# SwiGLU's last 1024 features mostly by seven products, and a last norm scaled on VectorE from PSUM

## The chip, the cores and the metric

One NeuronCore of a Trainium2 chip runs the whole step. The metric is device time in microseconds of one execution. The engines are TensorE (PE; PEld is its weight load), VectorE (DVE), ScalarE (ACT), GpSimd (POOL) and SyncE (SP, which only issues DMAs). All arithmetic is on float32 data; a float32 product is made of three matmuls on operands split into a high and a low part.

## What is computed

One step of a streaming encoder layer on 576 rows (512 of a prompt, 64 of a sample) of width 1024, the inner width of SwiGLU being 4096. The parts that the change touches are the two SwiGLUs and the last norm:

```python
def rmsnorm(x, g):
    y = xf * lax.rsqrt(jnp.mean(xf * xf, axis=-1, keepdims=True) + EPS)
    return y * g
def swiglu(x, w_in, w_out):
    a, b = jnp.split(x @ w_in, 2, axis=-1)
    return (jax.nn.silu(a) * b) @ w_out
# layer
x = x + 0.5 * swiglu(rmsnorm(x, norm_ffn1), w_ffn1_in, w_ffn1_out)
x = x + mixer(rmsnorm(x, norm_mix))        # SSD, band attention, mLSTM, gates, output projection
x = x + 0.5 * swiglu(rmsnorm(x, norm_ffn2), w_ffn2_in, w_ffn2_out)
y = rmsnorm(x, final_norm)
```

## The kernel before, in words

The state lies transposed in SBUF as eight tiles R of 128 features by 576 rows. A float32 operand is split (`split`, L288 and L289) into a rounded high part made by a cast on ScalarE and the rest, subtracted on VectorE; `ph` and `pl` are those of a weight, `XH`/`XL`, `YH`/`YL` and `TH`/`TL` those of data. Three matmuls, (high, high), (high, low) and (low, high), add up in PSUM.

There are two ways to multiply. The plain one (`gemm`, `matmuls`, L260) goes by output tiles of 128 features and two pieces of the rows, `HALVES`, of 256 and 320. The other (`stream`, `product`, L616) is a scheme with seven products in place of eight: a unit makes two output tiles by two halves of 288 rows from two halves of the inner dimension, out of sums of weight quarters (made by an accumulating DMA from GpSimd, L461, and GpSimd additions, L472) and sums of data halves (`operands`, `hidden_operands`). Each of the seven products has four pieces of 128 inner features by three matmuls of 288 columns, and each weight operand is a 128x512 split. `stream` interleaves the products of neighbouring units and prepares weight operands five products ahead; evacuations have a raised priority. Jobs in `jobs` (the splits of hidden tiles) run between products, one step at each `tick`.

`ffn` first makes four of the hidden tiles plainly and then streams: units of the input projection (`unit`, evacuated by `swiglu`, L627 to L643, into `g` tiles of 128x2x288), and, for each 1024 hidden features c = 0, 1, 2, four units `out(c, m)` of the output projection, evacuated by `residual` (L655) into R. For the last 1024 features (c = 3) the hidden tiles are split whole (`hidden_parts`, L681) into YH and YL, whose memory takes the place of the operand tiles T2 after `out(2, 3)` (`hidden_tiles`), and the output projection of these 1024 features is plain: `gemm` in two parts of 512 (`for i in (6, 7)`), evacuated by `evac_o` at L712. The first FFN ("a") ends with rows 0 to 255 and then 256 to 575; the last one ("c", `last=(1, 0)`) the other way round.

After the first FFN the mixer begins with `norm`: per feature tile XH on ScalarE (L338) and XL on VectorE (L339), squares on ScalarE (L296, L299) added up on VectorE (L300), column sums by TensorE (`total`, L314), the power on GpSimd (L306), a spread of the row scales over partitions by TensorE (`spread`, L330) and a copy to `rs` on ScalarE (L354). Plain X tiles of the mixer need only XH and XL; their evacuations (L600) and the seven-product operands (xk at L434, then xd and splits) need `rs`. Then come a gate tile (L1488) and transposes of gates (L794), and the mixer's seven-product units.

After the last FFN, `norm_out` takes the squares, sums and row scales for rows 256 to 575 first (h = 1), copies the spread scales to `rs` (L401) and multiplies the eight tiles at L422, four on VectorE and four on GpSimd. Rows 0 to 255 are transposed (L408), scaled by two engines from PSUM (L413 on VectorE, L415 on ScalarE) and stored row by row. Pools hand memory on from tag to tag: a tile that is allocated where another lay waits for the other's last reader. The scheduler lists each engine's instructions in an order fixed at build time.

Of the kernel before, what the change touches and what calls it, by code (L numbers as in the profile page):

```python
# [35 lines left out]
NB = 63  # L36
NS = 115
# [44 lines left out]
class Hybrid:  # L82
    def __init__(self, ctx, tc, I, O):
# [7 lines left out]
        self.b_i = 0  # L91
        self.jobs, self.gap, self.side = deque(), 0, iter(())
# [102 lines left out]
    def squares(self, tag):  # L195

        pool, bufs = self.sqp
        if pool is self.op:
            return self.op.tile([128, T], F32, name=bufs[tag], tag=bufs[tag], bufs=2)[:, :320]
        return pool.tile([128, 320], F32, name=tag, tag=tag, bufs=bufs[tag])  # L200
# [44 lines left out]
    def parts(self, src):  # L245
        return self.split(src, self.ring("ph", F32R), self.ring("pl", F32R))
# [133 lines left out]
    def norm_out(self, x, g0, out):  # L380

        nc = self.nc
        with self.tc.high_priority(offset=1500):
            for h in (1, 0):
# [25 lines left out]
        for i in range(4):  # L410
            o = self.ring("wr")
            if i % 2:
# [39 lines left out]
    def fetch_sums(self, desc):  # L452
# [5 lines left out]
        src = self.I["sblk"][i].rearrange("p (q c) -> p q c", q=4)  # L458
        x12 = self.ring("wx", shape=(128, 2, 512))
# [3 lines left out]
    def fetch(self, raw):  # L463

        for q in (2, 3, 0) if self.mixer else (0, 2, 3):
            raw[q] = self.ring("wr")
# [20 lines left out]
    def stream(self, seq, order, banks):  # L487
# [17 lines left out]
        for i, (n, t) in enumerate(uses):  # L505
# [11 lines left out]
            if t == self.T_X2:  # L517
                del raw[n], st[n]

    def pairs(self, seq):  # L520
# [26 lines left out]
        def pair(tiles, done):  # L547
# [20 lines left out]
            return (name, 0, c1, c2), self.T, on  # L568
# [40 lines left out]
    def product(self, ps, ops, moving, start):  # L609
# [3 lines left out]
        for kk in range(4):  # L613
            wsl = slice(kk * 128, (kk + 1) * 128)
            for i, (wt, xx) in enumerate(((hi, th), (hi, tl), (lo, th))):
                self.nc.tensor.matmul(ps, wt[:, wsl], xx[:, kk, :], start=(start and kk == 0 and i == 0),  # L616
                                      stop=(kk == 3 and i == 2), skip_group_check=True)
# [62 lines left out]
    def hidden_parts(self, slot, g):  # L680
        self.split(g.rearrange("p h t -> p (h t)"), self.YH[:, slot, :], self.YL[:, slot, :])  # L681
        yield 1

    def ffn(self, x, g0, win, wout, name, last=(0, 1)):

# [24 lines left out]
        def evac_o(ot):  # L710
            def go(h, ps, sl):
                nc.vector.scalar_tensor_tensor(x[:, ot, sl], ps, 0.5, x[:, ot, sl], op0=ALU.mult, op1=ALU.add)  # L712
# [3 lines left out]
        def at(c, j):  # L716
            return (8 * c + (j if c == 3 else j % 2 * 4 + j // 2)) * 128
# [22 lines left out]
        def flush():  # L740
# [3 lines left out]
            for c, j in sorted(got):  # L744
                if c == 3:
                    self.jobs.append(self.hidden_parts(j, got.pop((c, j))))
                elif j % 2 == 0 and (c, j + 1) in got:
                    self.jobs.append(self.hidden_operands(j // 2, got.pop((c, j)), got.pop((c, j + 1))))
# [3 lines left out]
        def unit(c, j):  # L752
# [3 lines left out]
            return (win, 0, 4096 + at(c, j), at(c, j)), self.T, self.swiglu(done)  # L756

        def out(c, m):
            def done():
                free[0] = True  # L760
                if c == 2:
                    self.hidden_tiles(name)
                flush()
            return (wout, 1024 * c, 256 * m, 256 * m + 128), self.T2, self.residual(x, m, done if m == 3 else None)
# [844 lines left out]
```

## Time and profile before

| what | value |
|---|---|
| runs of the kernel | 1943.83, 1940.4, 1938.6 us; median 1940.4 us |
| profiled execution, its own time | 1944.79 us |
| its span on the core | 1943.1 us |
| mean granted clock of TensorE | 0.991 |
| busy: PE, DVE, ACT, POOL | 1887.2, 1524.6, 1089.5, 680.1 us |

The profiled execution is one of many; its time lies a little above the median. Times in the rows are microseconds from the start of the span, unless marked ns. TensorE issues a matmul before the last one has left the array, so a matmul's own duration (about 0.3 us) is longer than the distance to the next. `x12` at a row's end counts instructions of one kind in a row; in brackets is the idle time of the engine before them, and what ended it.

### The profile page before, as it was taken

What the parts mean: (1) busy time and instruction counts of PE and PEld (TensorE: products, weight loads), DVE (VectorE), ACT (ScalarE), POOL (GpSimd) and SP (SyncE); (2) the same over time, 40 slices, a digit from 0 to 9 for tenths busy, and PEclk for the clock granted to TensorE, in tenths of its full rate; (3) what the DMA queues carried; (4) which work ended last, traced back from release to release, by engine and by line L of the source; (5) the groups of instructions that cost most, each with busy time, mean ns of one, the idle gap of its engine ahead of it and who ended that gap; (6) DMA issues with size and microseconds to landing.
All of it is one profiled execution on the core that took longest, in us unless ns stands there. A gap on an engine that the chain in (4) does not pass through costs nothing. (4 is left out here: it accounts for less than half of the span.)

```text
span 1943.1 us, 37678 instructions
## 1 busy us (share of the span) xinstructions
PE 1887.2 (97%) x13901; PEld 1823.6 (94%) x13901; DVE 1524.6 (78%) x2715; ACT 1089.5 (56%) x2486; POOL 680.1 (35%) x656
## 2 busy tenths in 40 slices
PE   9999999999999999999999998999999999999998
PEld 8899999999999878888888888999999999999998
DVE  8998998988768767667777775745898888988865
ACT  4554654655544777767675765324555455554544
POOL 5343333333202234323435353440233334334311
PEclk9999999999999999899999999999999999999999
DMA  7267666666742545753667557742236666666631
GB/s 241 74 160 173 159 163 163 159 172 163 185 131 80 156 117 159 200 147 108 183 165 183 155 152 213 241 143 88 77 99 165 163 157 172 166 157 167 159 94 60
DMA packets 129440, 294.69 MB, mean 152 GB/s; under 512 B 14289, under 2 KB 26193, under 8 KB 129257
## 3 DMA queue, kind: packets, MB, share of 16 engines
q1 hardware_dynamic: 100072, 205.67, 32.7%
q0 software_dynamic: 19696, 72.10, 20.5%
q10 hardware_dynamic: 9488, 14.53, 2.6%
q8 instruction: 109, 1.79, 0.4%
q14 instruction: 75, 0.61, 0.1%
HBM read 272.87 MB, written 19.38 MB: 150 GB/s over the span
## 5 line engine op out<-in xcount | busy, mean ns | idle before, releaser
L616 PE MATMUL acc<-TH,ph 128*128 128x288 f32 x3220 | 968.0, 301 | 27.4 <-ACT uv L533 11.8
L616 PE MATMUL acc<-TL,ph 128*128 128x288 f32 x3220 | 955.4, 297 | 0.6 <-DVE TL L289 0.6
L616 PE MATMUL acc<-TH,pl 128*128 128x288 f32 x3220 | 955.0, 298 | 1.0 <-DVE pl L289 0.9
L616 PEld LDWEIGHTS acc<-TH,ph 128*128 128x128 f32 x3220 | 607.5, 189 | 46.9 <-ACT uv L533 15.5
L616 PEld LDWEIGHTS acc<-TL,ph 128*128 128x128 f32 x3220 | 609.4, 189 | 4.9 <-issue 3.7
L616 PEld LDWEIGHTS acc<-TH,pl 128*128 128x128 f32 x3220 | 608.4, 189 | 4.8 <-DVE pl L289 2.2
L289 DVE TENSOR_TENSOR pl<-wr,ph 128x512 fp32r<-128x512 f32 x471 | 429.4, 919 | 76.9 <-ACT ph L288 64.5
L288 ACT CAST ph<-wr 128x512 fp32r<-128x512 f32 x471 | 287.9, 620 | 267.9 <-PE acc L616 141.3
L289 DVE TENSOR_TENSOR pl<-wx,ph 128x512 fp32r<-128x512 f32 x390 | 328.1, 845 | 44.5 <-ACT ph L288 37.9
L288 ACT CAST ph<-wx 128x512 fp32r<-128x512 f32 x390 | 237.4, 621 | 201.3 <-POOL wx L472 110.2
L472 POOL TENSOR_TENSOR wx<-wx,wr 128x512 f32<-128x512 f32 x160 | 246.3, 1539 | 188.2 <-DVE pl L289 150.4
L461 POOL DMA_DIRECT2D wx<-in_sblk x115 | 101.6, 901 | 524.1 <-DMA wx<-in_sblk 154.7
L260 PE MATMUL acc<-YH,ph 128*128 128x256 f32 (+1 forms) x768 | 226.5, 298 | 6.3 <-ACT YH L288 5.8
L260 PE MATMUL acc<-YL,ph 128*128 128x320 f32 (+1 forms) x768 | 227.1, 297 | 2.3 <-DVE YL L339 1.9
L260 PE MATMUL acc<-YH,pl 128*128 128x256 f32 (+1 forms) x768 | 226.5, 296 | 0.1
L260 PEld LDWEIGHTS acc<-YH,ph 128*128 128x128 f32 x768 | 145.4, 190 | 6.9 <-ACT YH L288 5.9
L260 PEld LDWEIGHTS acc<-YL,ph 128*128 128x128 f32 x768 | 145.4, 189 | 3.5 <-DVE YL L339 3.3
L260 PEld LDWEIGHTS acc<-YH,pl 128*128 128x128 f32 x768 | 145.2, 189 | 0.3 <-DVE pl L289 0.3
L472 POOL TENSOR_TENSOR wy<-wx,wr 128x512 f32<-128x512 f32 x35 | 56.2, 1605 | 136.0 <-DVE pl L289 120.0
L655 DVE SCALAR_TENSOR_TENSOR R<-acc,R 128x288 f32<-128x288 f32 x168 | 75.7, 450 | 18.6 <-PE acc L616 18.1
L288 ACT CAST TH<-g 128x288 fp32r<-128x288 f32 x120 | 51.6, 434 | 59.8 <-POOL g L641 34.6
L289 DVE TENSOR_TENSOR pl<-wy,ph 128x512 fp32r<-128x512 f32 x70 | 59.8, 857 | 29.6 <-ACT ph L288 26.6
(320 smaller groups left out, 2393.4 us busy)
## 6 DMA issues: line engine op xcount, KB each, us to landing
wr<-in_sblk SPq DMA_DIRECT2D x345, 256.0 KB, 3.6
wx<-in_sblk SPq DMA_DIRECT2D x115, 512.0 KB, 3.8
wx<-in_sblk POOLq DMA_DIRECT2D x115, 512.0 KB, 6.8
wr<-in_wblk SPq DMA_DIRECT2D x126, 256.0 KB, 3.0
R<-scr_rows ACTq DMA_DIRECT2D x12, 576.0 KB, 5.9
gs<-g SPq DMA_DIRECT2D x20, 288.0 KB, 4.5
g<-gs POOLq DMA_DIRECT2D x20, 288.0 KB, 3.9
y<-ys POOLq DMA_DIRECT2D x12, 288.0 KB, 3.8
```

Of the source, the lines that this page charges most:

```text
L260: nc.tensor.matmul(ps[:, :n], wt[:, wsl], xx[:, k0 + k, a:a + n], start=(k == 0 and i == 0), stop=(k == nk - 1 and i == 2))
L288: self.nc.scalar.copy(hi, src)
L289: self.nc.vector.tensor_tensor(lo, src, hi.bitcast(F32), op=ALU.subtract)
L461: return {"x12": x12, "src": src}, lambda: nc.gpsimd.dma_start(x12, src[:, 1:3, :], accum_op=ALU.add)
L472: add = lambda o, one, two: self.nc.gpsimd.tensor_tensor(o, one, two, op=ALU.add)
L616: self.nc.tensor.matmul(ps, wt[:, wsl], xx[:, kk, :], start=(start and kk == 0 and i == 0), stop=(kk == 3 and i == 2), skip_group_check=True)
L655: self.nc.vector.scalar_tensor_tensor(o, ps, scale, o, op0=ALU.mult, op1=ALU.add)
```

## The change

Of the last 1024 hidden features, 768 (six hidden tiles, three pairs) now go by seven products like the others: `out(3, m)`, four units with three pieces of 128 in each product (`product` takes their number from the operand's width; the weight quarters are 128x384, filled with zeros to 512 in HBM and loaded at 384). The other 256 (hidden tiles j = 6, 7) stay plain: `rest(m, n)` runs between the units, right behind the last product of each, with one 128x512 weight split in a unit (loaded into a `g` buffer) and four pieces of 288 columns of 6 matmuls; the banks are those of the stream. `hidden_parts` splits tiles 6 and 7 into piece 3 of the operand tiles of T_X1, T_A11, T_X4 and T_A22, which the three-piece products leave free. The pool of YH and YL is no longer opened in their place, so T2 lives until the end of the FFN. The plain `gemm` calls at the end are gone.

In `norm_out` the spread scales stay in PSUM, all eight multiplications of rows 256 to 575 are on VectorE, behind the last residual (`issue_after(self.final)`), and of the four last scalings one, not two, is on VectorE. The squares take buffers of the weights (`wr`) and of `g`.

```diff
@@ norm_out
                 if h:
                     self.total([acc], n, pt)
-                    ps, _ = self.spread(pt, n)
-                    rb = self.rs[:, :320]
-                    nc.scalar.copy(rb, ps[:, :n])
+                    rb = self.spread(pt, n)[0][:, :n]
...
-            if i % 2:
+            if i == 1:
                 nc.vector.tensor_scalar(o, tr[i], r[:, i // 2:i // 2 + 1], None, op0=ALU.mult)
...
         for k in range(8):
-            eng = nc.gpsimd if k % 2 else nc.vector
-            eng.tensor_tensor(x[:, k, sl], x[:, k, sl], rb, op=ALU.mult)
+            with self.tc.issue_after(self.final):
+                nc.vector.tensor_tensor(x[:, k, sl], x[:, k, sl], rb, op=ALU.mult)
@@ stream, product
+            if self.then:
+                self.then = self.then()
...
-        for kk in range(4):
+        nk = hi.shape[1] // 128
+        for kk in range(nk):
@@ hidden tiles
-    def hidden_parts(self, slot, g):
-        self.split(g.rearrange("p h t -> p (h t)"), self.YH[:, slot, :], self.YL[:, slot, :])
-        yield 1
+    def rest(self, k, h):
+
+        return [v[:, 3, :] for v in self.T2[(self.T_X1, self.T_A11, self.T_X4, self.T_A22)[2 * k + h]]]
+
+    def hidden_parts(self, k, g):
+        for h in range(2):
+            self.split(g[:, h, :], *self.rest(k, h))
+            yield 1
@@ ffn
+        def rest(m, n):
+
+
+            late.append(self.parts(raws.pop(0)))
+            if m < 2:
+                todo = [(m, e, h) for e in range(2) for h in range(2)]
+            else:
+                todo = [(g, e, h) for h in last for g in (2, 3) for e in range(2) if (g == 2 and h == last[0]) == (m == 2)]
...
+            for g, e, h in todo:
+                hi, lo = late[g]
+                ps = self.half_bank(banks.pop())
+                for k in range(2):
+                    th, tl = self.rest(k, h)
+                    wsl = slice(k * 256 + e * 128, k * 256 + e * 128 + 128)
+                    for i, (w, t) in enumerate(((hi, th), (hi, tl), (lo, th))):
+                        nc.tensor.matmul(ps, w[:, wsl], t, start=(k == 0 and i == 0), stop=(k == 1 and i == 2))
+                evac_o(2 * g + e)(h, ps, slice(h * FH, (h + 1) * FH))
+
+        def out(c, m, n=None):
             def done():
+                if c == 3:
+                    self.then = partial(rest, m, n)
+                    return
                 free[0] = True
-                if c == 2:
-                    self.hidden_tiles(name)
                 flush()
...
+        seq += [out(3, m, len(seq) + m) for m in range(4)]
...
-        for i in (6, 7):
-            tiles = [((wout, i * 512, 512, j * 256, 256), [(0, evac_o(2 * j)), (128, evac_o(2 * j + 1))])
-                     for j in range(4)]
-            n = 1 if i == 7 else 4
-            self.gemm(tiles[:n], self.YH, self.YL, k0=(i % 2) * 4)
-            self.gemm(tiles[n:], self.YH, self.YL, k0=(i % 2) * 4, half_major=True, order=last)
+        self.sqp = self.wp, None
```

The scheduler puts the instructions in an order of its own. Where the first FFN ends and the mixer's norm begins, VectorE's list before reads as follows (L712 are the residuals of the plain tiles, L339 the XL of the mixer, L289 subtractions of weight splits, L300 sums of squares):

```order
L339 SCALAR_TENSOR_TENSOR XL<-R_60,cst,XH 128x320
L712 SCALAR_TENSOR_TENSOR R_60<-acc,R_60 128x320
L289 TENSOR_TENSOR pl<-wr,ph 128x512
L712 SCALAR_TENSOR_TENSOR R_60<-acc,R_60 128x320
L339 SCALAR_TENSOR_TENSOR XL<-R_60,cst,XH 128x320
L289 TENSOR_TENSOR pl<-wr,ph 128x512
L300 TENSOR_TENSOR xd<-xd,xk 128x256 x2
```

And after, where the same steps are L727 (residuals of `rest`), L663 (residuals of the units), L345 (XL), L295 and L306:

```order
L727 SCALAR_TENSOR_TENSOR R_60<-acc,R_60 128x288 x2
L295 TENSOR_TENSOR pl<-wr,ph 128x512
L727 SCALAR_TENSOR_TENSOR R_60<-acc,R_60 128x288 x2
L295 TENSOR_TENSOR pl<-wr,ph 128x512
L345 SCALAR_TENSOR_TENSOR XL<-R_60,cst,XH 128x256 x2
L306 TENSOR_TENSOR xd<-xd,xk 128x256
L345 SCALAR_TENSOR_TENSOR XL<-R_60,cst,XH 128x256 x2
L306 TENSOR_TENSOR xd<-xd,xk 128x256
L345 SCALAR_TENSOR_TENSOR XL<-R_60,cst,XH 128x256 x4
```

Before, XL and residuals alternate; after, the XL stand behind the last residual.

On TensorE, the list at the same place goes before from the plain tiles of YH to those of XH:

```order
L260 MATMUL acc<-YH,ph 128x320
L260 MATMUL acc<-YL,ph 128x320
L260 MATMUL acc<-YH,pl 128x320
L260 MATMUL acc<-XH,ph 128x256
L260 MATMUL acc<-XL,ph 128x256
L260 MATMUL acc<-XH,pl 128x256
```

After, from the last piece of `rest` (L803; the operand tiles TH_907 to TL_910 are those that hold hidden tiles 6 and 7) to the X tiles:

```order
L803 MATMUL acc<-TH_907,ph 128x288
L803 MATMUL acc<-TL_908,ph 128x288
L803 MATMUL acc<-TH_907,pl 128x288
L803 MATMUL acc<-TH_909,ph 128x288
L803 MATMUL acc<-TL_910,ph 128x288
L803 MATMUL acc<-TH_909,pl 128x288
L266 MATMUL acc<-XH,ph 128x256 x3
L266 MATMUL acc<-XL,ph 128x256
L266 MATMUL acc<-XH,pl 128x256
```

The X matmuls follow directly in both. Counted in the lists, the second spread of the norm (L330, after: L336) stands behind 118 matmuls of X tiles before, and behind 172 after.

At the kernel's end, VectorE's list before (L422 the scalings of rows 256 to 575, L305 and L325 first steps of the power, L413 the last scalings):

```order
L712 SCALAR_TENSOR_TENSOR R_60<-acc,R_60 128x256
L300 TENSOR_TENSOR na<-na,sq 128x256 x2
L712 SCALAR_TENSOR_TENSOR R_60<-acc,R_60 128x256
L300 TENSOR_TENSOR na<-na,sq 128x256 x2
L712 SCALAR_TENSOR_TENSOR R_60<-acc,R_60 128x256
L300 TENSOR_TENSOR na<-na,sq 128x256 x2
L422 TENSOR_TENSOR R_60<-R_60,rs 128x320 x4
L712 SCALAR_TENSOR_TENSOR R_60<-acc,R_60 128x256
L305 TENSOR_SCALAR sm<-ps_x 128x2
L413 TENSOR_SCALAR wr<-acc,sm 128x512 x2
```

And after (L426 the scalings, L311 and L331 the first steps, L417 the last scaling):

```order
L663 SCALAR_TENSOR_TENSOR R_60<-acc,R_60 128x288
L727 SCALAR_TENSOR_TENSOR R_60<-acc,R_60 128x288 x2
L306 TENSOR_TENSOR wr<-wr,g 128x320 x2
L306 TENSOR_TENSOR wr<-wr,g 128x256 x3
L311 TENSOR_SCALAR sm<-ps_x 128x2
L331 TENSOR_SCALAR sm<-ps_x 64x1
L306 TENSOR_TENSOR wr<-wr,g 128x256 x3
L426 TENSOR_TENSOR R_60<-R_60,ps_x 128x320 x8
L311 TENSOR_SCALAR sm<-ps_x 128x2
L417 TENSOR_SCALAR wr<-acc,sm 128x512
```

The last residual moved ahead of the scalings, of which there are eight, and the sums of squares stand behind it too.

## Rows read from the trace of the kernel before

**Rows 1.** Table of windows: PE, PEld, DVE, ACT, POOL busy, granted clock, DMA.
```profile
200.00:400.00 200.00, 199.67 (x1496) 199.21 (x1495) 182.93 (x282) 111.62 (x236) 76.27 (x68) 1.00 0.64 164
500.00:520.00 20.00, 20.00 (x152) 20.00 (x151) 17.32 (x24) 11.92 (x24) 6.00 (x6) 1.00 0.65 170
600.00:620.00 20.00, 20.00 (x152) 20.00 (x151) 20.00 (x36) 8.96 (x17) 6.98 (x4) 1.00 0.25 84
628.00:630.00 2.00, 2.00 (x11) 1.50 (x10) 2.00 (x5) 1.05 (x2) 0.00 (x0) 0.60 0.00 0
1880.00:1930.00 50.00, 50.00 (x377) 49.85 (x375) 27.34 (x58) 21.00 (x42) 2.15 (x3) 1.00 0.13 38
```

**Rows 2.** Chain of waits, its last 180 us: start, duration, engine, tile, line.
```profile
1763.66 110.58 PE acc L616 x828
1881.02 44.58 PE acc L260 x331
1925.60 0.55 PE ps_x L314 x6
1926.14 3.48 PE acc L260 x28
1929.63 0.82 PE ps_x L330 x6
1930.47 0.44 ACT rs L401
1930.97 4.39 POOL R L422 x4
```

**Rows 3.** The page's costliest groups, whole kernel: busy us, mean ns, idle before.
```profile
L289 DVE TENSOR_TENSOR pl<-wr,ph 128x512 fp32r<-128x512 f32 x471 | 429.4, 919 | 76.9 <-ACT ph L288 64.5
L289 DVE TENSOR_TENSOR pl<-wx,ph 128x512 fp32r<-128x512 f32 x390 | 328.1, 845 | 44.5 <-ACT ph L288 37.9
L472 POOL TENSOR_TENSOR wx<-wx,wr 128x512 f32<-128x512 f32 x160 | 246.3, 1539 | 188.2 <-DVE pl L289 150.4
L655 DVE SCALAR_TENSOR_TENSOR R<-acc,R 128x288 f32<-128x288 f32 x168 | 75.7, 450 | 18.6 <-PE acc L616 18.1
```

**Rows 4.** Groups of VectorE by line and shape, whole kernel.
```profile
L289 DVE TENSOR_TENSOR TL<-g,TH 128x288 fp32r<-128x288 f32 x120 | 56.7, 475 | 17.2 <-ACT TH L288 17.2
L289 DVE TENSOR_TENSOR YL<-g,YH 128x576 fp32r<-128x576 f32 x16 | 18.2, 1150 | 1.0 <-ACT YH L288 1.0
L339 DVE SCALAR_TENSOR_TENSOR XL<-R,cst,XH 128x320 fp32r<-128x320 f32 x8 | 4.4, 546 | 1.3 <-ACT XH L338 1.3
L712 DVE SCALAR_TENSOR_TENSOR R<-acc,R 128x320 f32<-128x320 f32 x32 | 15.6, 489 | 12.2 <-PE acc L260 12.1
```

**Rows 5.** Timeline of VectorE, 560 to 640 us: start us, duration us.
```profile
573.96 0.55 DVE L339 SCALAR_TENSOR_TENSOR XL<-R,cst,XH 128x320 fp32r<-128x320 f32 x1
574.42 0.48 DVE L712 SCALAR_TENSOR_TENSOR R<-acc,R 128x320 f32<-128x320 f32 x1
594.81 1.54 DVE L434 SCALAR_TENSOR_TENSOR xk<-R,cst,rs 128x576 f32<-128x576 f32 x2
628.41 0.45 DVE L289 TENSOR_TENSOR TL<-xk,TH 128x288 fp32r<-128x288 f32 x1
```

**Rows 6.** Timeline of TensorE at the hand-over and at the gates.
```profile
575.38 0.31 PE L260 MATMUL acc<-YH,pl 128*128 128x320 f32 x1
575.53 0.28 PE L260 MATMUL acc<-XH,ph 128*128 128x256 f32 x1
625.48 0.30 PE L794 MATMUL ps_x<-ident,R 24*128 24x24 f32 x2 [2.37 <-DVE R L1488]
```

**Rows 7.** Timeline of ScalarE, second copy of row scales in the mixer.
```profile
593.55 0.43 ACT L354 COPY rs<-ps_x 128x320 f32<-128x320 f32 x1 [1.79 <-PE ps_x L330]
```

**Rows 8.** Timeline of VectorE at the kernel's end.
```profile
1930.93 3.71 DVE L422 TENSOR_TENSOR R<-R,rs 128x320 f32<-128x320 f32 x4 [0.25 <-ACT rs L401]
1934.56 0.41 DVE L712 SCALAR_TENSOR_TENSOR R<-acc,R 128x256 f32<-128x256 f32 x1
```

More of the change, by code (lines that the diff above doesn't have):

```diff
@@ L35 @@
 CH = [(0, 128), (128, 128), (256, 128), (384, 128), (512, 64)]
-NB = 63
-NS = 115
+NB = 51
+NS = 123
 FH = 288
@@ L91, in __init__ @@
         self.b_i = 0
+        self.then = None
         self.jobs, self.gap, self.side = deque(), 0, iter(())
@@ L199, in squares @@
             return self.op.tile([128, T], F32, name=bufs[tag], tag=bufs[tag], bufs=2)[:, :320]
+        if pool is self.wp:
+            o = self.ring("wr") if tag == "na" else pool.tile([128, T], F32, name="g", tag="g", bufs=FBUFS["g"])
+            return o[:, :320]
         return pool.tile([128, 320], F32, name=tag, tag=tag, bufs=bufs[tag])
@@ L711, in go @@
             def go(h, ps, sl):
-                nc.vector.scalar_tensor_tensor(x[:, ot, sl], ps, 0.5, x[:, ot, sl], op0=ALU.mult, op1=ALU.add)
+                o = nc.vector.scalar_tensor_tensor(x[:, ot, sl], ps, 0.5, x[:, ot, sl], op0=ALU.mult, op1=ALU.add)
+                self.final = o.ins
             return go
         def at(c, j):
-            return (8 * c + (j if c == 3 else j % 2 * 4 + j // 2)) * 128
+            return (8 * c + (j if c == 3 and j > 5 else j % 2 * (3 if c == 3 else 4) + j // 2)) * 128
         boxes = [{} for _ in range(NPLAIN)]
@@ L744, in flush @@
             for c, j in sorted(got):
-                if c == 3:
-                    self.jobs.append(self.hidden_parts(j, got.pop((c, j))))
+                if c == 3 and j > 5:
+                    self.jobs.append(self.hidden_parts(j - 6, got.pop((c, j))))
+                    for m in (2 * j - 12, 2 * j - 11):
+                        w = self.wp.tile([128, T], F32, name="g", tag="g", bufs=FBUFS["g"])[:, :512]
+                        if m % 2 == 0:
+                            self.plan.append((wout, 3840, 256, m * 256, 512))
+                        nc.sync.dma_start(w, self.I["wblk"][len(self.plan) - 1][:, m % 2 * 512:m % 2 * 512 + 512])
+                        raws.append(w)
                 elif j % 2 == 0 and (c, j + 1) in got:
+                    if c == 3:
+                        self.jobs.append(iter((2,)))
                     self.jobs.append(self.hidden_operands(j // 2, got.pop((c, j)), got.pop((c, j + 1))))
@@ L755, in done @@
                 flush()
-            return (win, 0, 4096 + at(c, j), at(c, j)), self.T, self.swiglu(done)
-        def out(c, m):
+            return (win, 0, 4096 + at(c, j), at(c, j), 4), self.T, self.swiglu(done)
+        raws, late = [], []
+        def rest(m, n):
[4 more added lines that the diff above has]
+                todo = [(g, e, h) for h in last for g in (2, 3) for e in range(2) if (g == 2 and h == last[0]) == (m == 2)]
+            banks = deque((n % 3, 4 + n % 2, 3, (n + 2) % 3) if m < 3 else
+                          (n % 3, 4 + n % 2, 3, (n + 2) % 3, 4 + (n + 1) % 2, (n + 1) % 3))
+            for g, e, h in todo:
[8 more added lines that the diff above has]
+        def out(c, m, n=None):
             def done():
+                if c == 3:
+                    self.then = partial(rest, m, n)
+                    return
                 free[0] = True
-                if c == 2:
-                    self.hidden_tiles(name)
                 flush()
-            return (wout, 1024 * c, 256 * m, 256 * m + 128), self.T2, self.residual(x, m, done if m == 3 else None)
+            return ((wout, 1024 * c, 256 * m, 256 * m + 128, 3 if c == 3 else 4), self.T2,
+                    self.residual(x, m, done if m == 3 or c == 3 else None))
         for j, box in enumerate(boxes):
```

26 lines of the change are left out of this document (16 added, 10 removed).

## The prediction

> **What bounds the kernel now.** I read the table of windows and the chain of waits first, at the places that the change touches, since a removed matmul is worth its issue interval only while TensorE stays fed. In the first feed-forward (FFN) TensorE is busy 199.67 of 200 us in 200 to 400 us and all of 500 to 520 [rows 1]; in the last FFN the chain is one unbroken run of 828 seven-product matmuls in 110.58 us, and then 44.58 us of plain ones [rows 2]. So both places are TensorE's. Only after 1930 us does the chain pass to ScalarE and GpSimd [rows 2]. The third place is the start of the mixer: from 600 to 620 us VectorE is busy 20.00 of 20 us [rows 1], so there VectorE sets when the mixer's seven-product operands are ready.
>
> The profiled execution took 1944.79 us, above the median of 1940.4. I work with differences and put them on the median. A difference under about 0.3% (5.8 us) is what a measurement of this kernel can't tell from no change.
>
> **Matmuls removed.** A matmul of 288 columns takes 110.58/828 = 0.1336 us, a plain one (256 and 320 columns mixed) 44.58/331 = 0.1347 with the few transposes and sums between them [rows 2]; I take 0.1336 for all. For the last 1024 features, before issues 8 output tiles x 8 pieces of 128 x 3 products x 2 halves = 384; after issues 4 units x 7 x 9 = 252 and 4 x 24 = 96 plain, 348. So 36 fewer per FFN, 36 x 0.1336 = **4.81 us** each, 9.6 in all.
>
> **What must keep up.** One new unit with its plain part holds TensorE for 63 + 24 = 87 matmuls, 11.6 us. VectorE has seven subtractions of 384 columns (the means of the 512-wide ones, 0.919 and 0.845 us [rows 3], times 384/512: 3 x 0.689 + 4 x 0.634 = 4.6), seven evacuations at 0.450 [rows 3] = 3.15, the 512-wide subtraction of the plain part, 0.92, and four plain evacuations, 1.8: 10.5 us of 11.6. ScalarE's casts are shorter than VectorE's parts. Two GpSimd additions of 1539 x 384/512 = 1.15 us [rows 3] and one accumulating DMA more per unit go to an engine that was busy 2.15 of the last 50 us before 1930 [rows 1]; the queue of SyncE carries about the same bytes. Ahead of the units, VectorE makes three more sets of hidden operands, 21 subtractions at 0.475 and 15 plain ones at about 0.45, 16.7 us, in place of six YL of 1.150, 6.9 us [rows 4]: 9.8 us more in six units (67 us). The units of 200 to 400 us carry just this work, and there VectorE has 182.93 of 200 us and TensorE doesn't wait [rows 1]. I cost all this at nothing; TensorE covers it, with 1.1 us of slack per new unit.
>
> **The hand-over to the mixer, first FFN.** This is the price that I think the change pays. Before, the mixer's XH and XL are made while the last plain tiles still run: on VectorE an XL starts at 573.96, a residual at 574.42 [rows 5], and TensorE goes from the last YH matmul at 575.38 to the first XH one at 575.53 without a gap [rows 6]. After, the plain part reads two hidden tiles out of the seven-product operand tiles, which therefore stay allocated until the very last matmul, and XH and XL lie in that memory. The order shows the effect: on VectorE all sixteen XL stand behind the last residual. From the last FFN matmul on, I step through the order:
> - XH and XL of the first piece (about 0.5 us each, 546 ns on VectorE for one of 320 columns [rows 4]) come after the last matmul has left the array: TensorE idles some 1.7 us, give or take 0.5.
> - The squares for the norm start later too. TensorE spreads the second row of scales behind 172 matmuls of plain X tiles, where 118 stood before: 54 x 0.134 = 7.2 us later, and 1.7. The copy of that row came 593.55 - 575.53 = 18.0 us after the hand-over [rows 6, 7]; now it comes after 26.9.
> - That copy releases the first scaled operand (xk): 1.3 us later, so at 28.2 us; before at 594.81, 19.3 us [rows 5].
> - From there VectorE works without a pause to the last piece of the first product, the TL of 628.41 to 628.86 [rows 5], 34.0 us; with a few evacuations that now lie ahead of it taken off, 32.3. So 60.5 us against 53.3.
>
> TensorE has the same plain tiles to bridge this in both kernels. Before, they end in an idle of 2.37 us [rows 6] at the gates; after, they end some 7 us too early. The clock granted after the idle of before is 0.60 in 628 to 630 us [rows 1], the lower level (1.2 GHz) for most of it; after has that too, with an estimated 1 us more of it at most, half of those two microseconds. Price: 7.2 plus at most 1, I take **8.0**, of which 1.7 is the first wait. Against the 4.8, the first FFN loses 3.2 us.
>
> **The end of the kernel.** Before, the row scales are copied in 0.44 us, then GpSimd scales four tiles in 4.39 us [rows 2] and VectorE four in 3.71 [rows 8]. VectorE's block holds the last residual back to 1934.56 [rows 8]; its last matmul was 28 matmuls and a spread behind 1926.14 [rows 2], so some 3 us earlier. Behind it stand ScalarE's square, the sums, GpSimd's power, the last scalings and the store, which ends the span at 1943.1. After, eight scalings on VectorE stand behind the last residual. As halves of 288 columns don't match the norm's 256 and 320, both statistics now wait for the last pieces. From the last seven-product matmul, s: the last residual at s + 2.2 (six plain matmuls, 0.8, and a wait of 0.7 for a bank among them), sums, power and spread until s + 6.1, eight scalings at about 0.4 us each until s + 9.4, then VectorE's step for the other statistic, GpSimd, three ScalarE scalings until s + 12.2, store and end at s + 17.1, its tail as long as that of before. Matmuls alone would have ended at about 1930.2 before (1931.6 less sums and spread, 0.55 + 0.82 [rows 2]); 4.81 earlier is 1925.4, less the six plain ones s = 1924.7, and the end is 1941.8: **1.3 us gained** of the 4.8; the rest goes to the later statistics.
>
> What does a scaling cost? The rows show 3.71/4 = 0.93 us on VectorE while GpSimd works on the same tiles [rows 8], and an evacuation of 320 columns from PSUM 489 ns, begun every 0.4 us or so [rows 4]. I take the latter, the nearer form. At 0.93 the end would be 4 us later, 2.9 lost there. The Trainium skill (SBUF — State Buffer, section "SBUF: two separate sides") says that VectorE with two SBUF inputs and GpSimd reading SBUF share a port pair as an exclusive lock; by it the excess goes with GpSimd's share, and the sum would be the same. Against the change speaks the Trainium skill's Perfetto Trace Analysis, section "Optimizing Scalar/DVE Operations": about 125 ns of overhead for VectorE on PSUM, about 60 on SBUF; by it the eight scalings would be an estimated 0.5 us dearer than from SBUF. This trace doesn't show it: 489 ns for 320 columns with PSUM, 546 without [rows 4].
>
> **Sum.** +3.2 - 1.3 = +1.9 us: 1944.79 becomes 1946.7 in a like execution, the median 1940.4 becomes **1942.3 us**. The removed matmuls are paid back almost wholly at two ends that were hidden.
>
> **Rivals.**
> - *The ends hide after all.* If the mixer's operands don't set the pace as I stepped it (the chain of 32 us holds some 3 us of subtractions above their undisturbed length, and waits of TensorE further on in the mixer could absorb a shift), the gain stands: 9.6 and 0 to 1.3 at the end, about 1930; with half of it absorbed, 1936. For it: before, TensorE waits there only 2.37 us [rows 6]. Against: VectorE has no free microsecond in 600 to 620 [rows 1].
> - *VectorE becomes the bound in the new units (slower).* The 10.5 us of a unit hold only while a subtraction takes the mean of [rows 3]. It decides from 11.6 us on, 0.14 us more on each of the eight. With 12.4 us the eight units cost 0.8 x 8 = 6.4 us, and the total is 1948.7. For it: squares and GpSimd additions lie in the same stretch, and VectorE has 17.32 of 20 us already in 500 to 520 [rows 1]. Against: 828 such matmuls without a wait [rows 2], in a stretch with the same mix.
> - *The change does not do what it says.* The order rules most of it out: 36 matmuls fewer in each FFN, eight scalings on VectorE, none on GpSimd. 2%.
>
> **How the numbers follow.** My forecast, that both ends nearly even out: 0.53, with its own range of 1936 to 1947 (hand-over 4.5 to 9 us, end from 4 gained to 2.9 lost). The first rival 0.25, the second 0.20, the third 0.02. The range of 8 in 10 reaches into the first rival to 1931 and through the middle of the second to 1949. Faster by over 0.3% (below 1934.6): 0.25, the first rival but for its upper part, and the lower edge of mine. Slower by over 0.3% (above 1946.2): 0.22. Within: 0.53.
>
> **What would show it.** In the profile after: the chain of the last FFN unbroken at about 0.134 us a matmul and TensorE busy in full up to the hand-over (else the second rival); an idle of 1 to 2 us on TensorE at the first XH matmul; the second copy of row scales 25 to 28 us behind the last FFN matmul, against 18.0; TensorE idle for about 7 us near the first seven-product operands of the mixer; eight scalings at 0.4 to 0.5 us, and an end some 17 us behind the last seven-product matmul. I am wrong if that idle is missing, or if the mixer's later stages give the delay back.

## The result

The changed kernel takes 1947.27 us (median) where the kernel before takes 1941.25 in the same runs: a ratio of 1.003, interval 1.0023 to 1.0037, 6.0 us slower. A second measurement on another occasion gave 1.0036 (1.0023 to 1.0048). The forecast was 1.9 us slower and "within 0.3%"; the time lies inside the range, at the edge between "within" and "slower". The interval also shows that 0.3% can be told from no change here, other than the prediction took it. The direction and the places were right, one term was priced at nothing that costs 6 us, and one stage that I left out of the sum moved by some 4 us the other way; so it is partly luck that the time lies in the range.

The busy line of the page of after:

```profile
PE 1882.6 (97%) x13829; PEld 1815.4 (93%) x13829; DVE 1570.2 (81%) x2838; ACT 1099.3 (57%) x2552; POOL 694.3 (36%) x676
```

Its table of windows around the end of the first FFN (columns as in [rows 1]):

```profile
500.00:520.00 20.00, 19.73 (x148) 19.40 (x147) 16.35 (x30) 10.98 (x26) 8.01 (x7) 1.00 0.53 140
520.00:540.00 20.00, 18.28 (x134) 17.64 (x134) 19.22 (x32) 10.60 (x25) 7.27 (x8) 1.00 0.66 168
540.00:560.00 20.00, 19.23 (x143) 18.82 (x143) 17.44 (x36) 6.63 (x13) 4.83 (x5) 1.00 0.78 206
560.00:580.00 20.00, 18.41 (x131) 17.78 (x130) 15.77 (x34) 9.87 (x21) 2.37 (x3) 0.96 0.87 226
```

Before, TensorE had no idle time in the window 500 to 520 [rows 1] nor up to the hand-over. After, it waits in the units of the last 1024 features: 18.28 of 20 us between 520 and 540, with VectorE at 19.22. The timeline of after there, TensorE's rows first, then VectorE's, then GpSimd's:

```profile
522.62 0.40 PE L624 MATMUL acc<-TH,ph 128*128 128x288 f32 x1 [0.77 <-ACT P L640]
535.29 0.37 PE L624 MATMUL acc<-TH,ph 128*128 128x288 f32 x1 [0.47 <-ACT ph L294]
537.21 0.37 PE L624 MATMUL acc<-TH,ph 128*128 128x288 f32 x1 [0.48 <-DVE R L663]
553.65 0.37 PE L624 MATMUL acc<-TH,ph 128*128 128x288 f32 x1 [0.60 <-ACT ph L294]
...
529.59 0.45 DVE L663 SCALAR_TENSOR_TENSOR R<-acc,R 128x288 f32<-128x288 f32 x1
530.12 3.29 DVE L295 TENSOR_TENSOR pl<-wr,ph 128x384 fp32r<-128x384 f32 x1
551.14 1.99 DVE L295 TENSOR_TENSOR pl<-wr,ph 128x384 fp32r<-128x384 f32 x1
...
529.98 1.20 POOL L466 DMA_DIRECT2D wx<-in_sblk  x1 [4.36 <-DVE pl L295]
530.76 1.48 POOL L477 TENSOR_TENSOR wx<-wx,wr 128x384 f32<-128x384 f32 x1
531.74 1.25 POOL L649 TENSOR_TENSOR g<-g,P 128x288 f32<-128x288 f32 x1
```

One subtraction of 384 columns, 0.55 us when nothing disturbs it, holds VectorE for 3.29 us: it starts 0.14 us behind a GpSimd DMA issue and ends, an addition later, 0.42 us behind the end of a GpSimd multiplication (531.74 + 1.25 = 532.99; the subtraction ends at 533.41). Summing over all matmuls what an interval takes beyond 0.1336 us, TensorE loses 4.2 us at the end of the first FFN and 2.2 in the last; before, nothing in either.

At the hand-over the rows that answer to [rows 5 to 7], TensorE, ScalarE and VectorE of after:

```profile
576.49 1.00 PE L266 MATMUL acc<-XH,ph 128*128 128x256 f32 x3 [0.99 <-ACT XH L344]
577.97 0.39 PE L266 MATMUL acc<-XL,ph 128*128 128x256 f32 x1 [0.49 <-DVE XL L345]
...
604.49 0.42 ACT L360 COPY rs<-ps_x 128x320 f32<-128x320 f32 x1 [3.80 <-PE ps_x L336]
...
606.15 1.54 DVE L438 SCALAR_TENSOR_TENSOR xk<-R,cst,rs 128x576 f32<-128x576 f32 x2
...
635.53 0.53 PE L624 MATMUL acc<-TH,ph 128*128 128x288 f32 x2 [1.20 <-ACT TH L294]
637.88 0.61 PE L624 MATMUL acc<-TH,ph 128*128 128x288 f32 x1 [1.82 <-ACT TH L294]
```

Two windows of the same stretch, then one of before (the granted clock is the third number from the end):

```profile
575.00:585.00 10.00, 8.41 (x53) 7.78 (x52) 10.00 (x25) 9.35 (x23) 0.63 (x1) 0.83 0.74 232
635.00:645.00 10.00, 7.38 (x33) 6.75 (x33) 9.59 (x24) 6.92 (x14) 1.81 (x5) 0.66 0.24 76
...
625.00:635.00 10.00, 9.37 (x57) 8.35 (x58) 8.51 (x25) 4.20 (x8) 1.38 (x6) 0.83 0.11 35
```

The last FFN matmul is through at 575.34. The first XH matmul comes 1.15 us later, the second copy of row scales 29.1 us later (before 18.0), the first xk 30.8 (before 19.3). At the end of the kernel, the timeline of VectorE:

```profile
1925.56 0.46 DVE L727 SCALAR_TENSOR_TENSOR R<-acc,R 128x288 f32<-128x288 f32 x1 [0.66 <-PE acc L803]
1931.56 3.27 DVE L426 TENSOR_TENSOR R<-R,ps_x 128x320 f32<-128x320 f32 x8 [1.50 <-PE ps_x L336]
```

And the chain of waits of after there (rows as in [rows 2]):

```profile
1925.56 0.47 DVE R L727
1926.05 1.40 ACT g L305 x4
1927.49 0.43 DVE wr L306
...
1928.59 0.96 POOL sm L312
1929.55 0.53 POOL sm L332
```

The scalings cost 3.27/8 = 0.41 us each, as taken. But between the last residual and the first of them lie 5.5 us of squares, sums, power and spread, most of which ran under matmuls before.

### The profile page after: what moved, and what is told of

The parts are those of the page before. It is cut to its first block, busy times and chain, and to the rows that moved or that the text cites. A ratio compares the mean times of both kernels' runs of the same rounds, so it can differ in the third digit from the quotient of the medians.

```text
span 1942.5 us, 37822 instructions
## 1 busy us (share of the span) xinstructions
PE 1882.6 (97%) x13829; PEld 1815.4 (93%) x13829; DVE 1570.2 (81%) x2838; ACT 1099.3 (57%) x2552; POOL 694.3 (36%) x676
## 5 line engine op out<-in xcount | busy, mean ns | idle before, releaser
L624 PE MATMUL acc<-TH,ph 128*128 128x288 f32 x3388 | 1017.9, 301 | 31.8 <-ACT uv L540 11.0
L295 DVE TENSOR_TENSOR pl<-wr,ph 128x512 fp32r<-128x512 f32 (+1 forms) x463 | 433.2, 943 | 59.9 <-ACT ph L294 50.5
L294 ACT CAST ph<-wr 128x512 fp32r<-128x512 f32 (+1 forms) x463 | 278.3, 611 | 213.2 <-PE acc L624 130.6
L295 DVE TENSOR_TENSOR pl<-wx,ph 128x512 fp32r<-128x512 f32 (+1 forms) x422 | 344.0, 818 | 45.3 <-ACT ph L294 40.3
L294 ACT CAST ph<-wx 128x512 fp32r<-128x512 f32 (+1 forms) x422 | 251.8, 611 | 208.1 <-POOL wx L477 113.0
L477 POOL TENSOR_TENSOR wx<-wx,wr 128x512 f32<-128x512 f32 (+1 forms) x176 | 264.9, 1505 | 201.2 <-DVE pl L295 146.2
L266 PE MATMUL acc<-YH,ph 128*128 128x320 f32 (+1 forms) x512 | 151.8, 301 | 6.4 <-ACT YH L294 6.3
L266 PE MATMUL acc<-YL,ph 128*128 128x320 f32 (+1 forms) x512 | 152.9, 300 | 2.1 <-DVE YL L345 1.7
L266 PE MATMUL acc<-YH,pl 128*128 128x320 f32 (+1 forms) x512 | 151.6, 298 | 0.0
L663 DVE SCALAR_TENSOR_TENSOR R<-acc,R 128x288 f32<-128x288 f32 x224 | 100.6, 450 | 29.7 <-PE acc L624 29.4
L295 DVE TENSOR_TENSOR TL<-g,TH 128x288 fp32r<-128x288 f32 x158 | 74.9, 475 | 25.8 <-ACT TH L294 25.7
```

Source lines behind the costliest of these rows:

```text
L266: nc.tensor.matmul(ps[:, :n], wt[:, wsl], xx[:, k0 + k, a:a + n], start=(k == 0 and i == 0), stop=(k == nk - 1 and i == 2))
L294: self.nc.scalar.copy(hi, src)
L295: self.nc.vector.tensor_tensor(lo, src, hi.bitcast(F32), op=ALU.subtract)
L477: add = lambda o, one, two: self.nc.gpsimd.tensor_tensor(o, one, two, op=ALU.add)
L663: self.nc.vector.scalar_tensor_tensor(o, ps, scale, o, op0=ALU.mult, op1=ALU.add)
```

## Stages, over all profiles

A single execution varies by several microseconds, so the stages are laid side by side for all profiled kernels, each worked out from the timelines of TensorE: **A** from the first seven-product matmul of the first FFN to the fifth seven-product of the mixer (36 matmuls each), **of it E** from the last FFN matmul on, **M** from there to the first matmul of the stage that merges the mixer's branches (from there to C it is 208.6 to 209.9 us in all of them), **C** from the first seven-product matmul of the last FFN to the end of the span. **W** is the wait of TensorE in the units of the last 1024 features, first and last FFN.

| kernel | A | of it E | W first | M | C | W last | ratio to before |
|---|---|---|---|---|---|---|---|
| before | 586.2 | 76.5 | 0.0 | 564.5 | 517.8 | 0.0 | |
| e1: norm only | 586.9 | 76.5 | 0.0 | 558.8 | 517.7 | 0.0 | 1.0001 |
| e2: last FFN and norm only | 589.6 | 76.5 | 0.0 | 554.5 | 519.9 | 2.9 | 1.0002 |
| e3, e12: first FFN only | 597.1, 594.6 | 85.1, 83.5 | 4.4, 4.3 | 552.6, 552.7 | 516.6, 514.5 | 0.0 | 0.9997, 0.9999 |
| after, e5 | 594.6, 595.1 | 85.0 | 4.2, 4.0 | 552.7, 553.5 | 520.7, 520.4 | 2.2, 2.1 | 1.003, 1.0036 |
| e6: after, inputs padded | 595.3 | 84.9 | 4.7 | 553.1 | 520.3 | 2.5 | 1.0031 |
| e8: after, old norm | 594.1 | 84.9 | 3.7 | 552.3 | 521.1 | 2.2 | 1.0032 |
| e7: after, no additions | 589.2 | 83.5 | 0.1 | 555.7 | 518.5 | 0.1 | 0.9995 |
| e10: after, additions on VectorE | 589.0 | 83.3 | 0.8 | 553.0 | 517.1 | 0.2 | 1.0006 |
| e4: after, two pools | 592.6 | 79.8 | 4.9 | 558.1 | 519.3 | 2.3 | 1.0046 |
| e11: e10 and e4 | 587.8 | 80.1 | 0.6 | 563.6 | 518.0 | 0.4 | 1.0032 |
| e9: before, late hand-over | 593.9 | 84.0 | 0.0 | 562.3 | 517.6 | 0.0 | 1.0065 |

The early part of A (up to 200 us) varies by 3 us between executions of one program, so does C (e3, e12 and before have the same last FFN), and M of one program by 10 (before, e1 and e2 have the same mixer). W repeats within 1 us; conclusions rest on it, on E and on the ratios.

Two of these spreads go with TensorE's clock. E of one program is 85.1 in e3 and 83.5 in e12, and the granted clock around the first XH matmul is 0.75 there in the one and 1.00 in the other. M of before, e1 and e2 is 564.5, 558.8 and 554.5 at a mean granted clock of 0.982, 0.993 and 0.997. M times its granted clock, an estimate of M at full clock, is 554.3, 554.8 and 552.9 for these three, and 549.0 to 550.9 in the eight profiles of after, e3, e12, e5, e6, e7, e8 and e10, whose mixer has one and the same order of instructions.

## The experiments

**The parts alone.** e1 takes only the hunks of `norm_out`, e2 those and the new end of the last FFN, e3 (and e12, on another occasion) only the new end of the first FFN. The edit is a switch around the new end:

```diff
+        seven = {"a": False, "c": True}[name]
...
+                if c == 3 and not seven:
+                    self.jobs.append(self.hidden_whole(j, got.pop((c, j))))
...
+        if seven:
+            self.sqp = self.wp, None
+            return
```

> Both FFNs as before; only the last norm is new (eight scalings on VectorE from PSUM behind the last residual, three of the last four scalings on ScalarE). Theory: the scalings take 0.4 us each as after (3.27 us for eight), the last residual no longer waits behind a VectorE block of 3.71 us, and the end comes 1 to 2.5 us earlier: 1939 to 1940 against 1941.25. Rival, that the norm's new form is what costs at the end: 1 us or more later than before.

Measured 1.0001 (0.9986 to 1.0015). The block of VectorE is gone, as the timeline of e1 shows: the last residual comes directly ahead of the scalings, not behind them.

```profile
1929.40 0.42 DVE L732 SCALAR_TENSOR_TENSOR R<-acc,R 128x256 f32<-128x256 f32 x1 [1.05 <-PE acc L266]
1929.74 3.26 DVE L426 TENSOR_TENSOR R<-R,ps_x 128x320 f32<-128x320 f32 x8
```

The gain is small: the first step of the other statistic stands behind the eight on VectorE instead. The 1 to 2.5 us of the theory are not seen, though the interval doesn't exclude them.

> First FFN as before, last FFN and last norm new. Theory from the trace after: 4.8 us fewer matmuls, 1.9 us of TensorE waits in the new units, and a later end of the statistics; from 1815 us to the end the trace after lost 2.5 us against before, so 1941 to 1944. Rival, the prediction's own sum for the end: 1.3 us gained, 1940. Rival, that all of the loss lies in the first FFN: 1936 to 1938.

Measured 1.0002 (0.9990 to 1.0014). Beside 1941.25 the theory's 1941 to 1944 are 0.9999 to 1.0014, so what was measured is at their lower end; the rival of 1940 lies in the interval too, that of 1936 to 1938 doesn't. The stage itself (C) is 2.1 us longer than before.

> First FFN new, last FFN and last norm as before. Theory: TensorE waits of some 4 us in the new units eat the 4.8 us, and the late XH and XL put the mixer's seven-product operands some 7 us back, of which the mixer gives a part back: 3 to 8 us above before, 1944 to 1949. Rival, that the mixer's own waits absorb it all: within 1 us of before.

Measured 0.9997 (0.9984 to 1.0010), and, as e12:

> e3 once more, beside e9 on one chip. From the stages of the profiles (first FFN and hand-over 7.5 us late, 4 to 6 us of it given back in the mixer) the first FFN alone should cost 2 to 4 us, and e3's measurement, within 0.15% of before, was at the low end of its interval. Theory: 1.001 to 1.002. Rival, that the first FFN alone costs nothing and the two FFNs act on each other: 0.999 to 1.0005.

0.9999 (0.9989 to 1.0009): my theory fell both times. The first FFN alone costs nothing in the whole kernel, although A is 8 to 11 us longer. The mixer (M) gives a part of it back in the profiles: 552.6 us against 554.5 to 564.5, by the estimate at full clock some 4 us. Where the rest goes is not shown.

> The changed kernel itself, unaltered, beside others on one chip. The first FFN alone and the last FFN with the norm alone were each within 0.15% of before, the two together 0.3% above it. Theory, that the two parts act on each other or that their costs only show together: again 1.002 to 1.004 of before. Rival, that 0.3% was the measurement of one chip: within 0.1% of before.

1.0036 (1.0023 to 1.0048): the 0.3% is there.

> The same instructions as after in the same order; only the two weight inputs in HBM are longer (63 and 131 blocks in place of 51 and 123, the added ones unused), so that what lies behind them has other addresses. Theory, that the time comes from the instructions: the same as e5 within 0.1%. Rival, that the place of the data in HBM decides over the waits for DMAs, above all in the mixer: 2 to 6 us away from e5, in either direction.

```diff
-_INS = {"xT": (1024, T), "wblk": (NB, 128, 1024), "sblk": (NS, 128, 2048),
+_INS = {"xT": (1024, T), "wblk": (PB, 128, 1024), "sblk": (PS_, 128, 2048),
```

1.0031 (1.0021 to 1.0042), no difference that can be measured: the place of the data is not the cause.

> Both FFNs new, the last norm's scaling as before (the scales copied to SBUF, four tiles on VectorE, four on GpSimd). Theory, that the norm's new form is no loss (0.0 in e1): at the end the old form costs 1 to 3 us more, since both halves of the scaling now stand behind the last residual: 1 to 3 us above e5. Rival, that the new form is what costs in company of the new FFN: below e5 by 2 us or more.

1.0032 (1.0020 to 1.0044), the same as e5; the 1 to 3 us more of the theory are not seen. In the profile its end is 0.4 to 0.8 us longer (C of 521.1); the norm's form plays no part in the result.

**GpSimd's additions.** e7 leaves the additions of weight quarters in the three-piece units out (so four units of each FFN compute with wrong sums), e10 gives them to VectorE:

```diff
-            if t in (self.T_X3, self.T_X4):
+            if t in (self.T_X3, self.T_X4) and x12.shape[2] == 512:
```

```diff
-        add = lambda o, one, two: self.nc.gpsimd.tensor_tensor(o, one, two, op=ALU.add)
+        eng = self.nc.vector if x12.shape[2] == 384 else self.nc.gpsimd
+        add = lambda o, one, two: eng.tensor_tensor(o, one, two, op=ALU.add)
```

> After without the sixteen GpSimd additions of weight quarters in the three-piece units of both FFNs (the outputs that depend on them are not the reference's); every other engine has the same instructions in the same order. Theory, that GpSimd's work stretches VectorE's subtractions of the new units (one took 3.29 us) and thus makes TensorE wait: the long subtractions and most of the 4 us of waits from 515 to 555 us and of the 2 us in the last FFN go, and the time falls by 3 to 5 us against e5. Rival, that VectorE's own list is too long there: waits and time stay within 1 us of e5.

> After, with the sixteen additions of weight quarters in the three-piece units on VectorE instead of GpSimd; nothing is left out. Theory: each costs VectorE about 0.5 us, but no longer blocks it for 0.7 to 2.7 us, so the waits of TensorE in the new units of the first FFN fall from 4.3 to under 2 us and the time by 2 to 6 us against after: 1.000 to 1.0025 of before. Rival, that the load and not the blocking counts: as after or slower.

e7 gave 0.9995 (0.9981 to 1.0010), e10 1.0006 (0.9996 to 1.0015), 8 and 6 us below e5's ratio. The groups of VectorE by shape, first of after, then of e7, then of e10 (busy us, mean ns):

```profile
L295 DVE TENSOR_TENSOR pl<-wr,ph 128x384 fp32r<-128x384 f32 x24 | 20.6, 858 | 0.3
L295 DVE TENSOR_TENSOR pl<-wx,ph 128x384 fp32r<-128x384 f32 x32 | 18.9, 590 | 0.0
```

```profile
L295 DVE TENSOR_TENSOR pl<-wr,ph 128x384 fp32r<-128x384 f32 x24 | 13.3, 553 | 0.2
L295 DVE TENSOR_TENSOR pl<-wx,ph 128x384 fp32r<-128x384 f32 x32 | 17.7, 552 | 0.0
```

```profile
L295 DVE TENSOR_TENSOR pl<-wr,ph 128x384 fp32r<-128x384 f32 x24 | 13.3, 553 | 0.2
L295 DVE TENSOR_TENSOR pl<-wx,ph 128x384 fp32r<-128x384 f32 x32 | 18.2, 569 | 0.0
L478 DVE TENSOR_TENSOR wx<-wx,wr 128x384 f32<-128x384 f32 x16 | 8.8, 553 | 0.3 <-DMA wr<-in_sblk 0.2
```

The same 56 subtractions take 39.5 us beside GpSimd's additions and 31 without. Given the additions as well, VectorE has 8.8 us more of its own, hardly more in sum than it had, and TensorE's waits all but vanish (W of 4.2 and 2.2 becomes 0.8 and 0.2). The windows of e10 that answer to those of after:

```profile
520.00:540.00 20.00, 20.00 (x151) 19.79 (x150) 17.63 (x42) 10.74 (x24) 4.08 (x5) 1.00 0.73 184
540.00:560.00 20.00, 20.00 (x152) 20.00 (x151) 17.72 (x38) 6.78 (x13) 0.96 (x3) 1.00 0.88 231
```

So it is not the sum of VectorE's work that holds TensorE up, but GpSimd's additions: without them there W shrinks by 5.4 us, and the time by 4.7 us against after's ratio or 5.8 against e5's. This is the cause of the measured loss. (E of e7 and e10 is 1.6 us shorter as well, at a granted clock that stayed at 1.00; e12 has the same with the additions on GpSimd, so this is not put down to them.) How an addition comes to hold TensorE up, the profiles show in two ways. The first is a subtraction that VectorE can't finish: one of 512 columns at 518.65 takes 2.27 us beside an addition, ScalarE waits 3.29 us for the step of VectorE behind it, and TensorE then waits the 0.77 us at 522.62. The second goes by GpSimd's own list, and the 3.29 us of 530.12 hide it. The same place of the last FFN in after, GpSimd first, then VectorE, ScalarE, VectorE and TensorE:

```profile
1880.68 1.47 POOL L477 TENSOR_TENSOR wx<-wx,wr 128x384 f32<-128x384 f32 x1
1881.65 1.26 POOL L649 TENSOR_TENSOR g<-g,P 128x288 f32<-128x288 f32 x1
...
1880.03 0.56 DVE L295 TENSOR_TENSOR pl<-wr,ph 128x384 fp32r<-128x384 f32 x1
1882.94 0.43 ACT L294 CAST TH<-g 128x288 fp32r<-128x288 f32 x1 [2.95 <-POOL g L649]
1883.41 0.46 DVE L295 TENSOR_TENSOR TL<-g,TH 128x288 fp32r<-128x288 f32 x1 [2.82 <-ACT TH L294]
1885.21 0.37 PE L624 MATMUL acc<-TH,ph 128*128 128x288 f32 x1 [0.86 <-ACT ph L294]
```

Here the subtraction is through in 0.56 us, and TensorE waits all the same, longer than at 535.29. The multiplication that completes a hidden tile (L649) stands behind the addition on GpSimd, and ScalarE's casts and VectorE's next steps stand behind the multiplication. In all thirteen profiled ends of an FFN with the additions on GpSimd, this product starts 2.30 or 2.31 us behind the end of that multiplication; in ten of them VectorE stood idle for 2.8 to 3.7 us before it, with no subtraction held up. In e7, e10 and e11 it starts 2.6 to 3.0 us behind it, without a wait. In after, of the losses over a quarter of a microsecond, 2.9 us lie behind the late multiplication, 2.4 follow a held-up subtraction and 0.4 neither. Both ways start from the additions; no run takes them apart.

**The hand-over.** e4 frees the memory of XH and XL early: hidden tiles 6 and 7 go to operand tiles that lie higher, and these to a pool of their own, since the memory of the one pool stayed taken in the order until its last tile was done. e9 does the reverse to the kernel before:

```diff
-        return [v[:, 3, :] for v in self.T2[(self.T_X1, self.T_A11, self.T_X4, self.T_A22)[2 * k + h]]]
+        return [v[:, 3, :] for v in self.T2[(self.T_X3, self.T_A11, self.T_A21, self.T_X2)[2 * k + h]]]
...
+            self.hidden.enter_context(self.pools(name + "2", yq=dict(side="right")))
```

```diff
-            self.norm(x, C_GM, self.XH, self.XL)
+            with self.tc.issue_after(self.final):
+                self.norm(x, C_GM, self.XH, self.XL)
```

> After, but hidden tiles 6 and 7 lie in piece 3 of the operand tiles of T_X3, T_A11, T_A21 and T_X2, and these four are in a pool of their own, so that the memory of XH and XL comes free before the last plain matmuls. The work is the same. In the order the second spread of the norm then stands behind 116 matmuls of X tiles (118 before, 172 after). Theory, that the hand-over is what costs: the second copy of row scales comes about 18 us behind the last FFN matmul as before, not 23 or more, the idle at the first XH matmul (1.3 us) goes, and the time falls by 5 to 7 us to 1940 to 1942. Rival, that VectorE as the bound in the new units costs: 1945 to 1947 as after.

> Before, with one thing changed: the mixer's whole norm (XH, XL, squares) is held behind the last residual of the first FFN, as it is in after. No other work. In the order the second spread then stands behind 178 matmuls of X tiles (118 before, 172 after). Theory: the hand-over alone shows the late rows of after (second copy of scales at about 29 us, the mixer's first seven-product matmul at 53 to 54 us and its fifth product at about 85 us behind the last FFN matmul, before 18, 50.6 and 76.5), 8 us late there, and the mixer gives back about half: 3 to 5 us above before. Rival, that the mixer gives back all: within 1 us. Rival, that nothing is given back: 7 us or more.

> e10 and e4 together: additions on VectorE, and the memory of XH and XL free before the last plain matmuls. Theory: both causes of the first FFN's loss are smaller, by about 3 and 5 us at the mixer's first products; if the mixer doesn't take it back, 3 to 6 us below before, 1934 to 1937. Rival, from e4, where an earlier hand-over brought nothing: not faster than before.

TensorE and ScalarE of e4, then of e9:

```profile
578.19 0.30 PE L808 MATMUL acc<-TH,pl 128*128 128x288 f32 x1
578.32 0.28 PE L270 MATMUL acc<-XH,ph 128*128 128x256 f32 x1
...
598.97 0.43 ACT L364 COPY rs<-ps_x 128x320 f32<-128x320 f32 x1 [1.50 <-PE ps_x L340]
```

```profile
575.43 0.31 PE L260 MATMUL acc<-YH,pl 128*128 128x320 f32 x1
575.57 0.67 PE L260 MATMUL acc<-XH,ph 128*128 128x256 f32 x4
...
603.19 0.42 ACT L354 COPY rs<-ps_x 128x320 f32<-128x320 f32 x1
```

The rows go the way of the theories: with the memory free there is no gap at the first XH matmul, the scales come 20.7 us behind the hand-over (the theory had 18), and E falls from 85.0 to 79.8; with the norm held back in the kernel before, the scales come at 27.6 and E rises from 76.5 to 84.0. So the late norm makes most of E's 8.5 us: 5.2 of them go in e4, and alone it adds 7.5 in e9. The whole time does not follow, and the times that the three theories named all fell. e4 is at 1.0046 (1.0028 to 1.0064), above after, not below; e11 at 1.0032 (1.0020 to 1.0043), above e10. And e9 is at 1.0065 (1.0051 to 1.0079), 12.5 us for 7.5: a late start alone is not given back. A good part of the difference lies in M. It is 552.3 to 553.5 us in seven profiles of kernels with the hand-over of after, 555.7 in e7, but 558.1 and 563.6 in e4 and e11, 562.3 in e9; by the estimate at full clock 549.0 to 550.9, and 553.8, 558.0 and 557.1, where before's order has 552.9 to 554.8. All of these compute the same mixer, but each of these edits of the hand-over lets the scheduler write another order of the mixer's instructions (e4 and e11 share one), and by these profiles the order that came with the change is the quickest of the four. Whether it is the order, or the order together with the start, was not tried apart.

## Why the prediction came out as it did

- **Matmuls removed: right.** 36 fewer in each FFN, at 0.1336 us wherever TensorE isn't made to wait.
- **"I cost all this at nothing; TensorE covers it": wrong, and this is the step that failed.** It cost 4.2 us in the first FFN and 2.2 in the last, of which e10 wins 5.4 back. The sum of 10.5 us of 11.6 per unit was about right (VectorE's subtractions took 39.5 us for 56, 0.705 each, where I had 0.66), but a mean says nothing on a single wait: a product is held up when one operand is late, and the slack of 1.1 us per unit can't be saved for a delay of 2 or 3. GpSimd's additions I took as load on an idle engine; what they did was to stand in the way of VectorE's subtractions and of GpSimd's own multiplications. The means of [rows 3] held the signs: 0.845 and 0.919 us for an instruction that takes 0.68 when undisturbed (0.67 to 0.69 in the timelines of after; [rows 8] has the same between a VectorE and a GpSimd block). In the stretch of 200 to 400 us [rows 1] a product has four pieces, 12 matmuls to wait under; the new one has nine, with the same number of GpSimd additions. That this is why the waits show only here is argued, not shown. The second rival had the place and, by accident, the price (6.4 us), but put it down to too much load, which is not the cause.
- **Hand-over: right in place and mechanism, slightly small.** I stepped the scales to 26.9 us and xk to 28.2; they came at 29.1 and 30.8. The first idle was 1.15 us, not 1.7, but the granted clock behind it read 0.83 in 575 to 585 us, and 0.66 in 635 to 645. With before's 0.83 in 625 to 635 us set against it, an estimated 3.4 us of E's growth are the lower clock, for which I had 1 at most; the idle near the first seven-product operands is 5.7 us in five pieces, where I had named about 7, and before has 3.1 in two. E grew by 8.5 us where I took 8.0. Matmuls, waits and hand-over together made A 594.6 us against 586.2, and my +3.2 plus the waits is +7.4.
- **The mixer: not in the sum.** I assumed that it takes its shift along unchanged, and named as a sign of being wrong that later stages give the delay back. They give a part back: M of after is 6 us below the mean of the three kernels with the old order (559.3), and 4 by the estimate at full clock. The remark in the first rival, that waits further on could absorb a shift, falls with e9; the order changed under it.
- **The end: right in its steps, one of them too short, and without the waits.** I had 1.3 us gained. C of after is 520.7 against 517.8, 2.9 us lost; of the 4.2 between, 2.2 are waits in the units, and the rest is a longer tail: 18.7 us from the last seven-product matmul on (1923.75 to 1942.48) where I had 17.1. It is lost ahead of the scalings, which start 7.8 us behind that matmul where I had 6.1. e10, without the waits, has C at 517.1, 0.7 gained, less than C varies.

With 4.2 and 2.2 for the cover, my sum is 1.9 + 6.4 = 8.3 us where 6.0 was measured; with 0.5 for the hand-over, 1.6 for the tail and 4 to 6 off for the mixer it is 4.4 to 6.4. So the misses cancel in part, and the range held for that reason too. What stays open: by the ratios each FFN alone costs nothing (0.0 us give or take 2) and both together 6 to 7. The stages of the profiles (A up 8, M down 6 or, at full clock, 4, C up 2 to 3) add up to 4 to 7 for both, but to more than nothing for the first FFN alone. The intervals leave room for some of that; no run shows where the rest is. No kernel here is shown to beat before.

## What to carry to other kernels

Where one engine feeds another a product at a time, don't compare sums over a stretch: take each wait of the fed engine and follow it back through every engine's list. Do so also where a conspicuously long instruction stands close by: the one of 3.29 us here was not what its product waited for. Look at what GpSimd does at that moment, and at what its own list holds back. When units get shorter, count the GpSimd instructions per unit, and give VectorE what lies in the way, even if its sum of work rises. And a change that keeps memory longer moves the start of the next stage and its whole order; the order of the mixer was worth some 4 us or more here, most of what the change itself cost.

## What the runs showed of the hardware

- VectorE's subtraction of two SBUF operands stands still beside a GpSimd addition or multiplication. In after, 49 of the 56 subtractions of 384 columns took 0.54 to 0.56 us; the other seven, all beside an addition, took 1.21 to 3.29 and ended 0.41 to 0.43 us behind the end of the addition, or of the multiplication that followed it; in e10 two that started under a multiplication alone took 0.80 and ended 0.41 and 0.42 behind it. A DMA issue of GpSimd alone doesn't do it: at 540.99 us one took 0.54 us under an issue of 540.70 to 541.59. The Trainium skill (SBUF — State Buffer, section "Who interferes with whom") calls the port pair of the two engines an exclusive lock, and says that VectorE with two SBUF inputs contends with a GpSimd instruction that reads SBUF; the trace agrees, and shows that the waiting one can miss its turn: a subtraction that started at 1870.09, under an addition, ended behind a multiplication that started at 1870.81.
- At the hand-over, behind an idle time of TensorE of 0.99 us and one of 0.49 shortly after, the granted clock read 0.79 in these four microseconds, part of them at the lower level (1.2 GHz): the 256-column matmuls follow each other at 0.21 us, at 0.12 in e4, at the higher level (2.4 GHz). The same two idle times left the clock at 1.00 in e7, e10 and e12, of which e12 is the program of e3, where it fell. So these waits alone don't decide it. After, then e12, then matmuls of after:

```profile
576.00:580.00 4.00, 2.92 (x14) 2.51 (x15) 4.00 (x11) 4.00 (x12) 0.00 (x0) 0.79 1.04 308
578.50:582.50 4.00, 2.88 (x19) 2.48 (x20) 4.00 (x11) 4.00 (x12) 0.00 (x0) 1.00 1.03 321
...
578.71 0.42 PE L266 MATMUL acc<-XH,pl 128*128 128x256 f32 x1
578.92 0.41 PE L266 MATMUL acc<-XH,ph 128*128 128x256 f32 x1
```

- Reading the scales from PSUM was not dearer than SBUF: the eight scalings of 320 columns took 480 ns each as a mean (3.27 us in a row), and seven additions of the same shape with both operands in SBUF (L306) 486 in the same profile. The Trainium skill (Perfetto Trace Analysis, section "Optimizing Scalar/DVE Operations") would have an estimated 0.07 us more for each from PSUM (125 ns of overhead less 60); no run has the same eight scalings from SBUF without GpSimd beside them.
